# Where in a block of 512 bytes the high parts of one weight quarter begin: all four k-tiles at the stream's place, or the first two alone

## The chip, the core and the metric

The kernel runs on one core of one Trainium2 chip. The metric is the device time in microseconds of that core, from three executions: 716.06 us in the median, 715.36 to 717.12. A further execution was profiled and took 716.72 us; its span from the first to the last instruction is 714.9 us. All quoted times within the program are of that execution.

## The reference

The layer is one decoder block over 512 positions of width 1024, in float32. The half that the change touches is the feed-forward part:

```python
h = rmsnorm(x, norm2_g[l])
gu = h @ w_ffn_in[l]
g = causal_dwconv(gu[..., :D_FF], ffn_conv_w[l]) + ffn_conv_b[l]
x = x + (jax.nn.silu(g) * gu[..., D_FF:]) @ w_ffn_out[l]
```

with `D_FF = 2816`, so `w_ffn_in` is 1024 by 5632. Ahead of it stand a norm, an input projection, a short gated convolution, a sparse attention and a gated merge; the change touches nothing of them.

## The kernel before

**High and low parts.** TensorE reads each float32 operand as a rounded one (float32r). To keep accuracy, every operand is kept as a high part (the rounded value) and a low part (what is left), and every product is made of three matmuls: high weight by high data, high weight by low data, low weight by high data. `dense` (L400) issues, for one product over some k-tiles, first all pairs with the high weight (L403 with the high data, L404 with the low data, the same weights loaded for each) and then all with the low weight (L406). Each matmul has its own load of the stationary weights, a 128x128 block; the data stream through as the moving operand.

**The feed-forward part.** The 22 channel tiles of the gate and the 22 of the up projection are worked on in twos (`ff_strassen`). For two channel tiles and one of the two projections, `ff_forms` (L895) loads the two weight blocks and `ff_pair` (L939) makes the 2 by 2 block product in Strassen's form (Winograd's variant): seven products instead of eight, each of four k-tiles with half of the positions (256 columns). So one call of `ff_pair`, called a pair here, has 7 x 12 = 84 matmuls of 128x256, and there are 22 pairs. The data side, in seven combinations, lies ready in `xf_h` and `xf_l`. Of the weights, the lower right quarter (a22) is used as it is and has tiles of its own, `th` (high) and `tl` (low); a11 and a12 use a ring tile (`wh_s`, `wl_s`), and the four sums of quarters use `sh` and `sl`.

**The order in a pair.** The product with a22 comes first (called in L974): eight matmuls with `th`, two for each k-tile, and then four with `tl`. Then come a11, a12 and the sums. From the third pair on, two parts of the down projection (`pdn`, 24 matmuls of 128x512 each time) stand between one pair and the next, so that a pair is entered from the last matmuls of `pdn`.

**Where tiles lie.** The program sets every tile at a fixed byte in each partition. Written as the remainder by 512: the moving data `xf_h` and `xf_l` begin at 288, and since all their pieces are multiples of 512 bytes long, each stream of 256 columns begins at 288. The weights `tl`, `wh_s`, `wl_s`, `sh`, `sl` begin at 480, and each k-tile (128 columns, 512 bytes) likewise: 192 bytes further than the stream. The two buffers of `th` begin at 288, so that all four k-tiles of a22's high parts lie at the stream's place; a filler tile of 48 columns, `gap_w`, behind them takes the rest to 480. In `pdn` both sides lie at 480.

**Who makes the weights.** ScalarE writes `th` as a rounded copy of a22 and `tl` as its negative; a DMA of GpSimd's queue then adds the weights from memory onto `tl`, which leaves the rest (`dma_split`, L156). `p1` (L957, 256 columns) holds the product with a11: ScalarE copies it out of its bank (L976), and VectorE's first sum of the pair reads it (L954). It has two buffers. The order of instructions on every engine is set when the program is built, from the dependencies and a model of durations.

Of the kernel before, what the change touches and what calls it, by code (L numbers as in the profile page):

```python
# [11 lines left out]
F32 = mybir.dt.float32  # L12
F32R = mybir.dt.float32r
I32 = mybir.dt.int32
AF = mybir.ActivationFunctionType
ALU = mybir.AluOpType
AX = mybir.AxisListType

P = 128
D = 1024  # L20
# [62 lines left out]
def tile_block(ctx: ExitStack, tc: tile.TileContext, xT, pos, par, par2, w_tok, w_a3, w_gate, w_ao, w_bo, w_o,  # L83
               w_ff, w_dn, c_w1, out):
    nc = tc.nc
# [9 lines left out]
    def const(shape, name, dt=F32, pool=sb):  # L95
        return pool.tile(shape, dt, name=name, tag=name)
# [17 lines left out]
    def s_bank(name):  # L114
        return bank("s", name, 3)

    def t_bank(name):
        return bank("t", name, 2)

    def o_bank(name):  # L120
        return bank("o", name, 1)
# [29 lines left out]
    def split(h, l, v):  # L151
        hi = nc.scalar.activation(h, v, AF.Copy)  # L152
        nc.vector.tensor_sub(l, v, h.bitcast(F32))  # L153
        return hi

    def dma_split(h, l, raw, src, dst=None):  # L156

        nc.scalar.activation(h, raw, AF.Copy)  # L158
        nc.scalar.activation(l, raw, AF.Copy, scale=-1.0)  # L159
        nc.gpsimd.dma_start(l if dst is None else dst, src, accum_op=ALU.add)  # L160

    def ring(name):
        return (wf.tile([P, D], F32R, name=f"wh_{name}", tag="wh", bufs=NWF),
                wf.tile([P, D], F32R, name=f"wl_{name}", tag="wl", bufs=NWF))

    def raw_tile(name):
        return wf.tile([P, D], F32, name=f"wr_{name}", tag="wr", bufs=NRAW)
# [232 lines left out]
    def dense(acc, units, first=True, last=True):  # L400

        for i, (wh, wl, xh, xl) in enumerate(units):
            nc.tensor.matmul(acc, wh, xh, start=first and i == 0, stop=False)  # L403
            nc.tensor.matmul(acc, wh, xl, start=False, stop=False)  # L404
        for i, (wh, wl, xh, xl) in enumerate(units):
            nc.tensor.matmul(acc, wl, xh, start=False, stop=last and i == len(units) - 1)  # L406
# [412 lines left out]
    TH = S // 2  # L819
# [6 lines left out]
    xf_h = const([P, 4, 7, TH], "xf_h", F32R, px)  # L826
    xf_l = const([P, 4, 7, TH], "xf_l", F32R, px)
    pw = ctx.enter_context(tc.tile_pool(name="pw", bufs=1, side="left"))
    pw.tile([P, D // 2], F32R, name="th_", tag="th", bufs=2)
    const([P, 48], "gap_w", F32, pw)  # L830

    def x_forms(k, v):
# [6 lines left out]
    for n, j in enumerate(O_ORDER):  # L839
# [10 lines left out]
        k, half = j % 4, j // 4  # L850
        if half == 0:
            v = pc.tile([P, 7, TH], F32, name=f"xv{k}", tag="xv", bufs=2)
        nc.scalar.activation(v[:, 2 * half:2 * half + 2].rearrange("p a t -> p (a t)"), xj, AF.Copy,
                             scale=par_sb[:, G2 + j:G2 + j + 1])
# [38 lines left out]
    HALF_D = D // 2  # L893

    def ff_forms(f, n):  # L895

        nm = f"{n}_{f}"
        raws = []
        for m in range(2):
            raw = raw_tile(f"s{nm}{m}")  # L900
            nc.sync.dma_start(raw, w_ff[f + m, n])
            raws.append(raw)
        a11, a12 = raws[0][:, 0:HALF_D], raws[0][:, HALF_D:]
        a21, a22 = raws[1][:, 0:HALF_D], raws[1][:, HALF_D:]
        form = {}
        h = pw.tile([P, HALF_D], F32R, name=f"th{nm}", tag="th", bufs=2)
        l = pw.tile([P, HALF_D], F32R, name=f"tl{nm}", tag="tl", bufs=2)
        dma_split(h, l, a22, w_ff[f + 1, n][:, HALF_D:])
        form["a22"] = (h, l)
        h, l = ring(f"s{nm}")  # L910
        dma_split(h, l, raws[0], w_ff[f, n])
        form["a11"] = (h[:, 0:HALF_D], l[:, 0:HALF_D])
        form["a12"] = (h[:, HALF_D:], l[:, HALF_D:])

        def put(i, j, v):
            h = pw.tile([P, D], F32R, name=f"sh{i}{j}{nm}", tag="sh", bufs=NSQ)
            l = pw.tile([P, D], F32R, name=f"sl{i}{j}{nm}", tag="sl", bufs=NSQ)
            split(h, l, v)
            form[i] = (h[:, 0:HALF_D], l[:, 0:HALF_D])
            form[j] = (h[:, HALF_D:], l[:, HALF_D:])  # L920

        s = {}

        def pair(i, j):
            v = pw.tile([P, D], F32, name=f"s{i}{j}{nm}", tag="sf", bufs=NSF)
            s[i], s[j] = v[:, 0:HALF_D], v[:, HALF_D:]
            return v

        v = pair(2, 3)
        nc.vector.tensor_sub(s[3], a11, a21)  # L930
        nc.vector.tensor_sub(s[2], a22, s[3])
        put(2, 3, v)
        v = pair(4, 1)
        nc.vector.tensor_sub(s[4], a12, s[2])
        nc.vector.tensor_add(s[1], a21, a22)
        put(4, 1, v)
        return form

    def ff_pair(f, n, c, form, late=None):  # L939
        nm = f"{n}_{f}"  # L940
        b1, b26 = o_bank(f"p1{nm}"), t_bank(f"p26{nm}")
        b45, b37 = s_bank(f"p45{nm}"), s_bank(f"p37{nm}")
        lo, hi = slice(0, TH), slice(TH, S)

        def units(wf_, x, ks):
            wh, wl = form[wf_]
            return [(wh[:, k * P:(k + 1) * P], wl[:, k * P:(k + 1) * P], xf_h[:, k, x], xf_l[:, k, x]) for k in ks]

        def product(acc, wf_, x):
            dense(acc, units(wf_, x, range(4)))  # L950

        def sums(dst, bank, v):

            nc.vector.tensor_tensor(dst, bank.rearrange("p (a t) -> p a t", a=2), v[:, None, :].to_broadcast([P, 2, TH]),  # L954
                                    op=ALU.add)

        p1 = pw.tile([P, TH], F32, name=f"p1{nm}", tag="p1", bufs=2)  # L957
        c1, c2 = c[:, :, 0:TH], c[:, :, TH:]
        plan = [(b26, hi, 2, T2, True), (b37, hi, 3, T3, True), (b37, lo, 4, B22, False), (b45, hi, 1, T1, True),
                (b1, lo, "a11", B11, True), (b26, lo, "a12", B21, False), (b45, lo, "a22", T4, False)]  # L960
        if late is not None:

            for b, cols, wf_, x, opens in plan:
                for i, (wh, wl, xh, xl) in enumerate(units(wf_, x, range(3))):
                    for lhs, rhs, st in ((wh, xh, True), (wh, xl, False), (wl, xh, False)):
                        nc.tensor.matmul(b[:, cols], lhs, rhs, start=opens and st and i == 0, stop=False,
                                         skip_group_check=True)

            def product(acc, wf_, x):
                (wh, wl, xh, xl), = units(wf_, x, (3,))  # L970
                for lhs, rhs, last in ((wh, xh, False), (wh, xl, False), (wl, xh, True)):
                    nc.tensor.matmul(acc, lhs, rhs, start=False, stop=last, skip_group_check=True)

        product(b45[:, lo], "a22", T4)  # L974
        product(b1[:, lo], "a11", B11)
        nc.scalar.activation(p1, b1[:, lo], AF.Copy)  # L976
        product(b26[:, lo], "a12", B21)
        product(b26[:, hi], 2, T2)
        sums(c1, b26, p1)
        product(b37[:, hi], 3, T3)  # L980
        product(b37[:, lo], 4, B22)
        sums(c2, b37, c1[:, 1])
        product(b45[:, hi], 1, T1)
        sums(c[:, 1].rearrange("p (a t) -> p a t", a=2), b45, c2[:, 1])
        nc.vector.tensor_add(c2[:, 0], c2[:, 0], b45[:, hi])
# [3 lines left out]
    def ff_strassen(f, between):  # L989
        u = u_bufs[f // 2 % NU]  # L990

        with tc.high_priority(offset=AHEAD if f == 0 else 0):
            form = ff_forms(f, 0)
        ff_pair(f, 0, u[:, :, 2:], form, late=f == 0 or None)
        between()
        nc.vector.tensor_tensor(u[:, :, 2:], u[:, :, 2:], r2two, op=ALU.mult)
        cv = pair_tile(f"cv{f}", "cv")
        for m in range(2):
            conv_silu(f + m, cv[:, m], u[:, m])
        nc.vector.tensor_tensor(cv, cv, r2two, op=ALU.mult)  # L1000
        up = pair_tile(f"up{f}", "up")
        ff_pair(f, 1, up, ff_forms(f, 1))

        between()
        nc.vector.tensor_tensor(up, up, cv, op=ALU.mult)
        for m in range(2):
            h, l = a_tiles(f + m)
            split(h, l, up[:, m])
# [98 lines left out]
```

## Time and profile before

| What | Value |
|---|---|
| Time, median of three executions | 716.06 us (715.36 to 717.12) |
| Profiled execution: its own time, its span | 716.72 us, 714.9 us |
| TensorE busy | 708.9 us, 99% of the span, 4285 matmuls |
| ScalarE, VectorE, GpSimd busy | 432.6, 534.7, 181.9 us |
| Matmuls of 128x256 of the pairs | 84 x 22 = 1848, from 365 to 684 us |
| Granted TensorE clock, mean over the span | 0.999 |

Busy time of TensorE says little here: matmuls overlap in the records (a 128x256 one lasts 0.28 us, but the next starts 0.12 us later), so what a matmul costs is the distance from its start to the start of the next, called its step below. Steps can be read off the timeline, whose starts are given to 0.01 us, best over many matmuls at once. The duration of one matmul is a second reading: a matmul that was held up lasts some nanoseconds longer.

### The profile page before, as it was taken

The page shows a single profiled execution, that of the slowest core. Times are in us where ns is not written, and L with a number is a line of the kernel's source. Part 1 is how long each engine was busy: PE and PEld are TensorE (multiplying, and loading weights), DVE is VectorE, ACT ScalarE, POOL GpSimd, SP SyncE. Part 2 cuts the span into 40 slices and gives each one's busy share as a digit, 9 for nine tenths or more (in the row PEclk, how much of TensorE's full clock was granted, in tenths as well). Part 3 has the DMA queues.
Part 4 walks back from the last instruction along what each step waited for, and adds up shares of the span by engine and source line. Part 5 has one row for each costly group of instructions (what it writes and reads, how often), then busy time and mean ns, then how long its engine had stood idle before and what let it go on. Part 6 is the DMA issues. An engine that isn't in the chain of part 4 may idle for free.

```text
span 714.9 us, 11371 instructions
## 1 busy us (share of the span) xinstructions
PE 708.9 (99%) x4285; PEld 633.4 (89%) x4285; DVE 534.7 (75%) x957; ACT 432.6 (61%) x722; POOL 181.9 (25%) x179
## 2 busy tenths in 40 slices
PE   9999999999999999999999999999999999999997
PEld 9999777888888888888789999899999999999986
DVE  6887876687566878365795899988787877878643
ACT  7535655967667676522676776676565766646440
POOL 3151332133433334433012221221211222111110
PEclk9999999999999999999999999999999999999999
DMA  7333677611111122332676798987878778785665
GB/s 273 97 95 118 173 179 154 143 60 60 60 64 55 60 69 80 118 125 82 206 201 136 172 234 202 220 203 187 206 188 216 170 185 198 188 206 105 122 142 150
DMA packets 41142, 105.47 MB, mean 148 GB/s; under 512 B 3968, under 2 KB 9216, under 8 KB 41088
## 3 DMA queue, kind: packets, MB, share of 16 engines
q1 hardware_dynamic: 26528, 70.41, 29.9%
q0 software_dynamic: 14272, 34.08, 27.7%
q8 instruction: 33, 0.54, 0.3%
q10 hardware_dynamic: 288, 0.26, 0.1%
q14 instruction: 21, 0.17, 0.1%
HBM read 102.64 MB, written 2.10 MB: 147 GB/s over the span
## 4 chain that ended last, share of the span: by engine, by line
PE 95%; DMA 2%; ACT 1%; DVE 1%; issue 1%; POOL 1%; ACTq 0%; DVEq 0%; POOLq 0%; SPq 0%
PE p L404 9%; PE p L403 9%; PE p L406 9%; PE pdn L404 6%; PE pdn L403 6%; PE pdn L406 6%; PE pg L404 4%; PE pg L403 4%; PE pg L406 4%; PE pa L403 2%; PE pt L679 2%; PE pa L404 2%; PE pa L406 2%; PE po L403 2%; PE po L404 2%; PE pj_s L253 2%
## 5 line engine op out<-in xcount | busy, mean ns | idle before, releaser
L404 PE MATMUL p<-xf_l,sh 128*128 128x256 f32 x336 | 80.6, 277 | 0.0
L403 PE MATMUL p<-xf_h,sh 128*128 128x256 f32 x336 | 80.5, 277 | 0.0
L152 ACT ACTIVATE sh<-s 128x1024 fp32r<-128x1024 f32 x44 | 46.2, 1057 | 38.0 <-PE p L404 24.5
L404 PE MATMUL pdn<-al,wh_d 128*128 128x512 f32 x176 | 68.7, 391 | 0.0
L403 PE MATMUL pdn<-ah,wh_d 128*128 128x512 f32 x176 | 68.5, 390 | 0.0
L404 PEld LDWEIGHTS p<-xf_l,sh 128*128 128x128 f32 x336 | 63.0, 188 | 0.1
L403 PEld LDWEIGHTS p<-xf_h,sh 128*128 128x128 f32 x336 | 63.0, 188 | 0.1
L160 POOL DMA_DIRECT2D wl_s<-in_w_ff_dram x22 | 19.5, 885 | 166.8 <-ACT wl_s L159 155.6
L153 DVE TENSOR_TENSOR sl<-s,sh 128x1024 fp32r<-128x1024 f32 x44 | 53.6, 1221 | 8.7 <-ACT sh L152 8.7
L158 ACT ACTIVATE wh_s<-wr_s 128x1024 fp32r<-128x1024 f32 x22 | 23.3, 1059 | 53.1 <-PE pdn L404 50.3
L406 PE MATMUL p<-xf_h,sl 128*128 128x256 f32 x336 | 51.5, 277 | 0.0
L135 POOL TENSOR_TENSOR wl_g<-wr_g,wh_g 128x1024 fp32r<-128x1024 f32 x16 | 38.4, 2402 | 50.8 <-ACT wh_g L133 25.4
L403 PE MATMUL pg<-xg_h,wh_g 128*128 128x512 f32 x128 | 50.7, 396 | 0.0
L404 PE MATMUL pg<-xg_l,wh_g 128*128 128x512 f32 x128 | 50.6, 395 | 0.0
L406 PE MATMUL pdn<-ah,wl_d 128*128 128x512 f32 x176 | 47.7, 389 | 0.0
L160 POOL DMA_DIRECT2D wl_d<-in_w_dn_dram x22 | 26.5, 1203 | 77.9 <-ACT wl_d L159 69.8
L1026 DVE TENSOR_TENSOR x<-x,pdn 128x512 f32<-128x512 f32 x48 | 32.9, 685 | 16.2 <-PE pdn L406 15.5
L406 PEld LDWEIGHTS p<-xf_h,sl 128*128 128x128 f32 x336 | 44.5, 188 | 0.2
L403 PE MATMUL p<-xf_h,wh_s 128*128 128x256 f32 x168 | 40.5, 276 | 0.0
L404 PE MATMUL p<-xf_l,wh_s 128*128 128x256 f32 x168 | 40.4, 276 | 0.0
L406 PEld LDWEIGHTS pdn<-ah,wl_d 128*128 128x128 f32 x176 | 33.0, 188 | 6.9
L404 PEld LDWEIGHTS pdn<-al,wh_d 128*128 128x128 f32 x176 | 33.0, 188 | 6.2
(359 smaller groups left out, 2121.8 us busy)
## 6 DMA issues: line engine op xcount, KB each, us to landing
wr_s<-in_w_ff_dram SPq DMA_DIRECT2D x44, 512.0 KB, 5.0
wl_s<-in_w_ff_dram POOLq DMA_DIRECT2D x22, 512.0 KB, 7.8
wr_d<-in_w_dn_dram SPq DMA_DIRECT2D x22, 512.0 KB, 7.3
wl_d<-in_w_dn_dram POOLq DMA_DIRECT2D x22, 512.0 KB, 8.6
wr_g<-in_w_gate_dram SPq DMA_DIRECT2D x16, 512.0 KB, 3.4
wr_a<-in_w_a_dram SPq DMA_DIRECT2D x12, 512.0 KB, 4.3
tl<-in_w_ff_dram POOLq DMA_DIRECT2D x22, 256.0 KB, 7.6
wl_a<-in_w_a_dram POOLq DMA_DIRECT2D x10, 512.0 KB, 7.6
```

Source lines behind the costliest of these rows:

```text
L135: e.tensor_sub(lo[:, 0:n], raw[:, 0:n], hi[:, 0:n].bitcast(F32))
L152: hi = nc.scalar.activation(h, v, AF.Copy)
L153: nc.vector.tensor_sub(l, v, h.bitcast(F32))
L158: nc.scalar.activation(h, raw, AF.Copy)
L160: nc.gpsimd.dma_start(l if dst is None else dst, src, accum_op=ALU.add)
L253: nc.tensor.matmul(acc, xg_h[:, k, ts_], wh, start=k == 0, stop=False)
L403: nc.tensor.matmul(acc, wh, xh, start=first and i == 0, stop=False)
L404: nc.tensor.matmul(acc, wh, xl, start=False, stop=False)
L406: nc.tensor.matmul(acc, wl, xh, start=False, stop=last and i == len(units) - 1)
L679: nc.tensor.transpose(pt[:, i * P:(i + 1) * P], e[:, i, (kt + k0) * P:(kt + k0 + 1) * P], ident)
L1026: nc.vector.tensor_add(xj, xj, acc)
```

## The change

The buffers of `th` grow from 512 to 640 columns, and the high parts are written into them in two pieces: k-tiles 0 and 1 in the first 256 columns, then a hole of 48 columns (192 bytes), then k-tiles 2 and 3. With the buffers still beginning at 288, k-tiles 0 and 1 stay at the stream's place, and k-tiles 2 and 3 begin at 480, where all other weights of the pairs begin. The 1024 bytes that two larger buffers take are given back by `p1`, which has one buffer instead of two; everything between `th` and `p1` moves up by 1024 bytes, a multiple of 512. The call of `dma_split` is written out, since the high part's access now has two pieces and the low part's has one.

```diff
-    pw.tile([P, D // 2], F32R, name="th_", tag="th", bufs=2)
+    pw.tile([P, 5 * P], F32R, name="th_", tag="th", bufs=2)
     const([P, 48], "gap_w", F32, pw)
...
-        h = pw.tile([P, HALF_D], F32R, name=f"th{nm}", tag="th", bufs=2)
+        h = pw.tile([P, 5 * P], F32R, name=f"th{nm}", tag="th", bufs=2)
         l = pw.tile([P, HALF_D], F32R, name=f"tl{nm}", tag="tl", bufs=2)
-        dma_split(h, l, a22, w_ff[f + 1, n][:, HALF_D:])
+        step = 2 * P + 48
+        h = h[:, 0:2 * step].rearrange("p (a c) -> p a c", c=step)[:, :, 0:2 * P]
+        nc.scalar.activation(h, a22.rearrange("p (a c) -> p a c", a=2), AF.Copy)
+        nc.scalar.activation(l, a22, AF.Copy, scale=-1.0)
+        nc.gpsimd.dma_start(l, w_ff[f + 1, n][:, HALF_D:], accum_op=ALU.add)
         form["a22"] = (h, l)
...
-            return [(wh[:, k * P:(k + 1) * P], wl[:, k * P:(k + 1) * P], xf_h[:, k, x], xf_l[:, k, x]) for k in ks]
+            high = lambda k: wh[:, k // 2, k % 2 * P:(k % 2 + 1) * P] if wf_ == "a22" else wh[:, k * P:(k + 1) * P]
+            return [(high(k), wl[:, k * P:(k + 1) * P], xf_h[:, k, x], xf_l[:, k, x]) for k in ks]
...
-        p1 = pw.tile([P, TH], F32, name=f"p1{nm}", tag="p1", bufs=2)
+        p1 = pw.tile([P, TH], F32, name=f"p1{nm}", tag="p1", bufs=1)
```

The order of instructions is the same on all engines; only the access of one instruction differs, and, with the single buffer of `p1`, some of the waits. On ScalarE, around the a22 copy for the gate projection of channel tiles 8 and 9, it stands before (`p10_6` in the output is `p1` of an earlier pair, `th0_8` and `tl0_8` are a22's tiles, `wr_s0_81` the raw weights):

```order
L976 ACTIVATE p10_6_4709<-p10_6_4705 128x256
L891 ACTIVATE cv4_4500<-cv4_4500 128x512
L158 ACTIVATE th0_8_5016<-wr_s0_81_5014 128x512
L159 ACTIVATE tl0_8_5017<-wr_s0_81_5014 128x512
L158 ACTIVATE wh_s1_6_4855<-wr_s1_60_4846 128x1024
L159 ACTIVATE wl_s1_6_4856<-wr_s1_60_4846 128x1024
```

and with the change:

```order
L982 ACTIVATE p10_6_4709<-p10_6_4705 128x256
L892 ACTIVATE cv4_4500<-cv4_4500 128x512
L911 ACTIVATE th0_8_5016<-wr_s0_81_5014 128x2x256
L912 ACTIVATE tl0_8_5017<-wr_s0_81_5014 128x512
L158 ACTIVATE wh_s1_6_4855<-wr_s1_60_4846 128x1024
L159 ACTIVATE wl_s1_6_4856<-wr_s1_60_4846 128x1024
```

The copy to `th` stands in the same place and writes the same 512 columns, now as two runs of 256; nothing ahead of it or behind it has moved.

## The prediction

> **What bounds the kernel now.** I read first the page's busy times and its chain of waits:
>
> ```profile
> PE 708.9 (99%) x4285; PEld 633.4 (89%) x4285; DVE 534.7 (75%) x957; ACT 432.6 (61%) x722; POOL 181.9 (25%) x179
> PE 95%; DMA 2%; ACT 1%; DVE 1%; issue 1%; POOL 1%; ACTq 0%; DVEq 0%; POOLq 0%; SPq 0%
> ```
>
> TensorE is never short of work, and 95% of the chain that ends last is its own. So the steps of the matmuls, start to start, make the time. Next I read the groups of TensorE by shape, for the 205 us in which pairs and down projection alternate, and the sums of that window:
>
> ```profile
> L403 PE MATMUL p<-xf_h,sh 128*128 128x256 f32 x224 | 53.5, 276 | 0.0
> L404 PE MATMUL p<-xf_l,th 128*128 128x256 f32 x56 | 13.9, 282 | 0.0
> L403 PE MATMUL p<-xf_h,th 128*128 128x256 f32 x56 | 13.9, 281 | 0.0
> 478.90:683.90 205.00, 205.00 (x1490) 192.51 (x1489) 157.39 (x218) 121.87 (x161) 39.83 (x40) 1.00 0.77 179
> ```
>
> Here 224 matmuls, 16 of each pair, are 14 pairs. TensorE is busy for all 205 us at a granted clock of 1.00. With equal shapes, matmuls whose weights are `th`, at the stream's place, last 281 or 282 ns; those with weights 192 bytes further last 276. Taken alone, that says: move `th` away and gain. The timeline says more. One of the 14 pairs, from its first `th` to the first `pdn` behind it (columns: start, duration):
>
> ```profile
> 554.06 0.28 PE L403 MATMUL p<-xf_h,th 128*128 128x256 f32 x1
> 554.18 0.28 PE L404 MATMUL p<-xf_l,th 128*128 128x256 f32 x1
> 554.30 0.28 PE L403 MATMUL p<-xf_h,th 128*128 128x256 f32 x1
> 554.41 0.28 PE L404 MATMUL p<-xf_l,th 128*128 128x256 f32 x1
> 554.54 0.28 PE L403 MATMUL p<-xf_h,th 128*128 128x256 f32 x1
> 554.65 0.28 PE L404 MATMUL p<-xf_l,th 128*128 128x256 f32 x1
> 554.77 0.28 PE L403 MATMUL p<-xf_h,th 128*128 128x256 f32 x1
> 554.89 0.28 PE L404 MATMUL p<-xf_l,th 128*128 128x256 f32 x1
> 555.01 0.62 PE L406 MATMUL p<-xf_h,tl 128*128 128x256 f32 x4
> ...
> 563.62 0.39 PE L403 MATMUL pdn<-ah,wh_d 128*128 128x512 f32 x1
> ```
>
> And one earlier pair, in which seven of the eight `th` matmuls had run before some `pdn`, and one alone led into the rest:
>
> ```profile
> 464.39 0.28 PE L404 MATMUL p<-xf_l,th 128*128 128x256 f32 x1
> 464.51 0.63 PE L406 MATMUL p<-xf_h,tl 128*128 128x256 f32 x4
> ...
> 473.46 0.39 PE L403 MATMUL pdn<-ah,wh_d 128*128 128x512 f32 x1
> ```
>
> From the first `tl` to `pdn` both hold the same 76 matmuls, whose weights all lie at 192 bytes behind the stream. They take 563.62 - 555.01 = 8.61 us behind eight `th`, and 473.46 - 464.51 = 8.95 us behind one: steps of 113.3 and 117.8 ns. So the same instructions, at the same addresses, have two paces, and each keeps to the end of the pair. Traffic does not part them: the windows (columns: length, TensorE busy and count, clock, DMA share, GB/s)
>
> ```profile
> 409.20:417.70 8.50, 8.50 (x78) 1.00 1.02 264
> 464.51:473.46 8.95, 8.95 (x78) 1.00 0.98 223
> 555.01:563.62 8.61, 8.61 (x78) 1.00 0.69 137
> ```
>
> show 113 ns with the DMA engines at 1.02 as with 0.69, and 118 at 0.98. What parts them is how the stretch was entered:
>
> ```profile
> 397.71 0.28 PE L403 MATMUL p<-xf_h,th 128*128 128x256 f32 x1
> 397.83 0.28 PE L404 MATMUL p<-xf_l,th 128*128 128x256 f32 x1
> 397.95 1.10 PE L406 MATMUL p<-xf_h,sl 128*128 128x256 f32 x8
> 398.89 0.28 PE L403 MATMUL p<-xf_h,th 128*128 128x256 f32 x1
> ...
> 399.48 0.28 PE L404 MATMUL p<-xf_l,th 128*128 128x256 f32 x1
> 399.61 0.62 PE L406 MATMUL p<-xf_h,tl 128*128 128x256 f32 x4
> 438.05 0.63 PE L403 MATMUL pdn<-ah,wh_d 128*128 128x512 f32 x2
> 438.51 1.10 PE L406 MATMUL p<-xf_h,sl 128*128 128x256 f32 x8
> ```
>
> Eight `sl` that last 1.10 us have steps of (1.10 - 0.28) / 7 = 0.117 us: two `th` ahead did not help, nor did two `pdn`. Six `th` (398.89 to 399.48) did: the four `tl` last 0.62 us, steps of (0.62 - 0.28) / 3 = 0.113. So `th` at the stream's place costs a little itself, and it is also what brings TensorE into the close pace, for the 76 matmuls behind it.
>
> **The change part by part.**
>
> *k-tiles 2 and 3 moved.* The direct effect is on the fifth to eighth `th`: 555.01 - 554.54 = 0.47 us now. At 113.3 ns they would take 0.45, at 117.8 again 0.47. A gain of 0.02 us in each pair, or none: at most 0.4 us in 22 pairs.
>
> *Whether four still do it.* One and two fail, six and eight succeed; the trace has no clean entry with four. The steps within the eight decide for me. From the starts they are 0.12, 0.12, 0.11, 0.13, 0.11, 0.12, 0.12, 0.12: not settled after four, where the widest step is directly followed by the narrowest, and level only at the end. Six behind 398.89 end in a wide step as well, 0.13 (399.61 - 399.48), so a wide step alone proves neither. But the fourth's is followed by a `th` that is itself held up, whereas the close pace begins behind a run that had levelled. I take it that four are too few. Where a stretch is not brought into the close pace it was never seen to come in by itself: the 464.51 stretch kept 117.8 ns for 76 matmuls. What leads into the first `th` is always the settled end of `pdn`, so the 14 pairs should all go one way.
>
> The price then: 8.95 - 8.61 = 0.34 us for a pair, 14 x 0.34 = 4.8 us. Before these pairs the close pace also held in
>
> ```profile
> 399.60:408.10 8.50, 8.50 (x77) 1.00 0.55 147
> 430.30:438.00 7.70, 7.70 (x70) 1.00 0.85 203
> ```
>
> and in the window at 409.20 above: 24.7 us, at 113.3 ns 218 matmuls, by 4.5 ns each 1.0 us. These entries are less clean, so between 0 and 1.0; I take 1.0, since they too rest on six or eight `th`. The sum is 4.8 + 1.0 = 5.8 us, less the 0.0 of the four moved ones. It lies wholly on the path, since TensorE has no idle time to give. The bounds are -0.4 us (close pace kept) and +5.8 us. A slower TensorE makes the other engines' deadlines later, so nothing new comes due.
>
> *The copy in two runs, and `p1` in one buffer.*
>
> ```profile
> L158 ACT ACTIVATE th<-wr_s x22: 613/617/637, 354.5 to 646.8; 128x512 fp32r<-128x512 f32 x22
> L976 ACT ACTIVATE p<-p x22: 357/361/385, 389.8 to 677.2; 128x256 f32<-128x256 f32 x22
> 419.86 0.68 DVE L954 TENSOR_TENSOR up<-p,p 128x512 f32<-128x512 f32 x1
> 422.79 0.36 ACT L976 ACTIVATE p<-p 128x256 f32<-128x256 f32 x1
> ```
>
> The copy writes the same 512 columns; it costs nothing more if the hole is free, and at most as much as two copies of 256, 2 x 361 - 617 = 105 ns, 2.3 us in all on an engine that is idle for 39% of the span. The last copy runs at 646.8, and the last `th` matmuls start at 675, 28 us later; even without that cover, 105 ns in 22 pairs would be 2.3 us. With one buffer, the write of `p1` waits for VectorE's read of the pair before; queued behind it on ScalarE are the copies that make weights. The closest case is the one above: the read ends at 420.54 and the write starts at 422.79, 2.25 us of room. Both edits cost nothing; no DMA is added, moved or resized, and no other remainder by 512 changes.
>
> **The rivals.**
>
> *Four are enough.* For it: the fourth `th` ends in a wide step, as the eighth does, and the shift comes in a rhythm that could have the same place after four as after eight. Against it: the fifth step is narrow although its weights still lie at the stream's place, and is followed by more wide ones, so the walk goes on. It would give 14 to 22 pairs x 0.02 us = 0.3 to 0.4 us less, 715.7 us. This is the one that ends on the other side. It decides by the step behind the fifth `th`: 113 ns there and in the 76 behind.
>
> *Only the clean pairs go wide, or the pace comes in late.* If a pair found the close pace halfway, it would lose 0.17 us, 14 x 0.17 = 2.4, and up to 0.5 us before: 718.5 to 719. Against it: no stretch at 117.8 ns was seen to come in without `th` or `pdn` ahead.
>
> *The addresses do nothing.* If the two paces came from something else, moving half of `th` would leave 716.1 us. Against it: 281 and 282 against 276 ns in the same 14 pairs. The Trainium skill, "TensorE: Matmul & The Clock Gate", section "Step-by-step: what each phase is for", states this rule: TensorE has two independent read ports, and loading the next weights takes no read bandwidth from the running matmul. By that rule no byte offset of a weight could matter, and the time would stay at 716.1 us. The trace speaks against it here, with 5 to 6 ns by offset alone.
>
> **How the numbers follow.** The profiled execution's 716.72 us would become 722.5; it stands 0.66 us above the median, so against the median of 716.06 the forecast is 716.06 + 5.8 = 721.9 us (own range 720.5 to 723.2: the 1.0 us of the early stretches may stay, and the runs shown spread by 1.8 us). Chances: four are too few 0.72; four are enough 0.20, at 715.7; the middle case 0.05, at 718.5 to 719; no effect 0.03. The range over these, so that no more than two in ten are left out, is 715.3 to 723.2 us. About 0.3%, 2.1 us, is what a measurement of this kernel can tell from no change. Slower by more: 0.72 and most of the middle case, 0.76. Faster by more would need the stretches that are wide now to come in as well. The longest are the 8.95 us above and
>
> ```profile
> 390.50:397.70 7.20, 7.20 (x63) 1.00 0.84 157
> 423.10:428.00 4.90, 4.90 (x42) 1.00 0.95 295
> ```
>
> 21 us in all; 4.5 ns of each 117.8 would be 0.8 us, with the 0.4 of `th` 1.2 us, under the bound: 0.02. The same: 0.22.
>
> **What would show it.** In the window of the 14 pairs, the groups with `sh`, `sl`, `wh_s`, `wl_s` and `tl` lasting 279 to 280 ns instead of 276, and 76 matmuls from the first `tl` to `pdn` in 8.95 us instead of 8.61, show the main step right; 276 and 8.61 show it wrong, and the rival right. The `th` groups of the second half at 279 or 280 go with it, at 276 with the rival. `pdn` should keep 388 to 391 ns. New idle time of ScalarE behind `p1`, or of TensorE at all, would show that the two small edits were mispriced. The forecast falls if the fifth `th` of a pair already steps by 113 ns.

## The result and the profile after

The changed kernel takes 722.33 us in the median of five executions (721.55 to 724.71); the kernel before took 716.33 us beside it (715.36 to 717.12). The ratio is 1.0085, with an interval of 1.0070 to 1.0099: slower by 6.0 us, 0.8%. The forecast was 721.9 us, with an own range of 720.5 to 723.2.

The profiled execution took 722.33 us, its span 720.6 us, 5.7 more than before. The page's busy times and its chain:

```profile
PE 714.1 (99%) x4285; PEld 638.2 (89%) x4285; DVE 535.3 (74%) x957; ACT 432.9 (60%) x722; POOL 182.4 (25%) x179
PE 95%; DMA 2%; DVE 1%; POOL 0%; ACT 0%; issue 0%; ACTq 0%; DVEq 0%; SPq 0%
```

TensorE is busy for 5.2 us more, with the same 4285 matmuls; VectorE, ScalarE and GpSimd stand within 0.6 us of before. The groups of TensorE from 480 to 690 us, which hold the 14 clean pairs (84 matmuls in one piece, each behind a whole `pdn`), and the sums of these pairs' window (length, TensorE busy and count, and at the end clock, DMA share, GB/s):

```profile
L403 PE MATMUL p<-xf_h,sh 128*128 128x256 f32 x224 | 55.3, 280 | 0.0
L404 PE MATMUL p<-xf_l,th 128*128 128x256 f32 x56 | 13.8, 280 | 0.0
L403 PE MATMUL pdn<-ah,wh_d 128*128 128x512 f32 x105 | 41.1, 392 | 0.0
479.89:689.64 209.75, 209.75 (x1490) 197.09 (x1489) 157.66 (x218) 122.12 (x161) 39.84 (x40) 1.00 0.76 175
```

`sh` lasted 276 ns before and lasts 280 now, although neither its place by 512 nor its order has changed. The window is 209.75 us long instead of 205.00, still without a gap in TensorE and at a clock of 1.00. One pair in the timeline (start, duration), its first `th`, the fifth to the eighth, `tl` and the first `pdn` behind it:

```profile
556.75 0.28 PE L403 MATMUL p<-xf_h,th 128*128 128x256 f32 x1
...
557.23 0.28 PE L403 MATMUL p<-xf_h,th 128*128 128x256 f32 x1
557.34 0.28 PE L404 MATMUL p<-xf_l,th 128*128 128x256 f32 x1
557.46 0.28 PE L403 MATMUL p<-xf_h,th 128*128 128x256 f32 x1
557.57 0.28 PE L404 MATMUL p<-xf_l,th 128*128 128x256 f32 x1
557.69 0.63 PE L406 MATMUL p<-xf_h,tl 128*128 128x256 f32 x4
...
566.64 0.40 PE L403 MATMUL pdn<-ah,wh_d 128*128 128x512 f32 x1
```

From the first `tl` to `pdn` the 76 matmuls take 566.64 - 557.69 = 8.95 us: the wide pace, 117.8 ns. The fifth `th`, the first one 192 bytes behind the stream, steps by 557.34 - 557.23 = 0.11 us. That is one close step; the three behind it, up to the first `tl`, take 557.69 - 557.34 = 0.35 us, 0.117 each, the wide pace.

Where the 5.7 us lie can be read off the first `th` of the first and of the last clean pair, in the timelines of before and of after:

```profile
478.93 0.28 PE L403 MATMUL p<-xf_h,th 128*128 128x256 f32 x1
674.27 0.28 PE L403 MATMUL p<-xf_h,th 128*128 128x256 f32 x1
```

```profile
479.92 0.28 PE L403 MATMUL p<-xf_h,th 128*128 128x256 f32 x1
679.68 0.28 PE L403 MATMUL p<-xf_h,th 128*128 128x256 f32 x1
```

The 14 pairs begin 0.99 us later than before. From the first to the last, 13 periods of a pair and its `pdn`, there are 195.34 us before and 199.76 after, 15.03 and 15.37 for each: 4.42 us more. The fourteenth pair adds 0.34. The sum is 0.99 + 4.42 + 0.34 = 5.75 us.

Of the 0.99 us ahead of them, 0.90 arise behind the first matmul of the pairs, which starts at 365.29 us before and at 365.38 now: they belong to the early stretches. All three that the prediction counted now begin with four `tl` at the wide pace, (0.63 - 0.28) / 3 = 0.117:

```profile
399.56 0.63 PE L406 MATMUL p<-xf_h,tl 128*128 128x256 f32 x4
409.44 0.63 PE L406 MATMUL p<-xf_h,tl 128*128 128x256 f32 x4
431.09 0.63 PE L406 MATMUL p<-xf_h,tl 128*128 128x256 f32 x4
```

### The profile page after: what moved, and what is told of

Read it like the earlier page. It is cut to its first block, busy times and chain, and to the rows that moved or that the text cites. A ratio compares the mean times of both kernels' runs of the same rounds, so it can differ in the third digit from the quotient of the medians.

```text
span 720.6 us, 11387 instructions
## 1 busy us (share of the span) xinstructions
PE 714.1 (99%) x4285; PEld 638.2 (89%) x4285; DVE 535.3 (74%) x957; ACT 432.9 (60%) x722; POOL 182.4 (25%) x179
## 4 chain that ended last, share of the span: by engine, by line
PE 95%; DMA 2%; DVE 1%; POOL 0%; ACT 0%; issue 0%; ACTq 0%; DVEq 0%; SPq 0%
PE p L403 10%; PE p L406 10%; PE p L404 10%; PE pdn L403 6%; PE pdn L404 6%; PE pdn L406 6%; PE pg L404 4%; PE pg L403 4%; PE pg L406 4%; PE pa L406 3%; PE pa L403 3%; PE pa L404 3%; PE pt L679 2%; PE po L403 2%; PE po L404 2%; PE pj_s L253 2%
## 5 line engine op out<-in xcount | busy, mean ns | idle before, releaser
L403 PE MATMUL p<-xf_h,sh 128*128 128x256 f32 x336 | 82.6, 280 | 0.0
L404 PE MATMUL p<-xf_l,sh 128*128 128x256 f32 x336 | 82.6, 279 | 0.0
L403 PEld LDWEIGHTS pdn<-ah,wh_d 128*128 128x128 f32 x176 | 33.0, 188 | 6.3
```

## The experiments

The theory of the prediction: out of the settled `pdn` (its 24 matmuls in one piece, with weights at the stream's place, as in the kernel before), a pair reaches the close pace only through a long run of matmuls whose weights lie at the stream's place, and four are too few. Its rivals: each matmul has its own price by its own offset (then moving `th` away gains); the loss comes from a side effect of the edit (the copy in two runs, the single `p1`, moved tiles). All times are medians of several executions, each beside executions of the kernel before on the same chip. "At the stream" counts the a22 matmuls of a pair whose weights lie at the stream's place.

| Kernel | At the stream, of 12 | Weights of `pdn` | Time, us | Ratio to before (interval) | Clean pairs at the wide pace |
|---|---|---|---|---|---|
| before | 8 | at the stream | 716.0 to 716.7 | 1 | 0 of 14 |
| the change | first 4 | at the stream | 722.33 | 1.0085 (1.0070 to 1.0099) | 14 |
| 1 no hole | 8 | at the stream | 716.33 | 1.0001 (0.9991 to 1.0011) | 0 |
| 2 all away | 0 | at the stream | 721.53 | 1.0076 (1.0061 to 1.0091) | 14 |
| 3 three k-tiles | first 6 | at the stream | 722.30 | 1.0090 (1.0070 to 1.0110) | 14 |
| 4 the two last | 4, later | at the stream | 721.63 | 1.0073 (1.0056 to 1.0090) | 14 |
| 7 eight, mixed | first 4 `th`, 4 `tl` | at the stream | 716.79 | 1.0008 (0.9996 to 1.0019) | 0 |
| 5 `pdn` away | 8 | 192 behind | 720.31 | 1.0055 (1.0040 to 1.0070) | 10 |
| 6 nothing at the stream | 0 | 192 behind | 716.84 | 1.0006 (0.9997 to 1.0016) | 0 |
| 8 four, `pdn` away | first 4 | 192 behind | 719.77 | 1.0043 (1.0025 to 1.0061) | 7 |
| 9 low data at the stream | 0 | 192 behind; with `al` at the stream | 723.73 | 1.0108 (1.0089 to 1.0126) | 14 |

The last column is counted from the mean step of the 72 matmuls behind the product with a22, pair by pair in the traces: it is 113.3 or 117.8 ns in every one of the 14 pairs of each kernel, never between. In kernels 3, 4 and 7 the order of some matmuls ahead of the 14 pairs differs from before too, so there the pace of the pairs says more than the total.

**1. The edit without the hole.** Everything of the change stays, the larger buffers, the copy with an access in two pieces, the single `p1`; the second piece follows the first directly.

```diff
-        step = 2 * P + 48
+        step = 2 * P
```

> The changed kernel with its larger tile, its copy written out as two runs and its single buffer of p1, but without the hole of 48 columns: all four k-tiles of th are at the stream's place again. Lead-in theory (eight th at the stream's place bring TensorE into the close pace, four do not): as before, 716 us, tl and sums lasting 276 ns. Side-effect theory (the single buffer of p1 or the written-out copy made the time): as the changed kernel, 722 us.

Measured: 716.33 us, the time before. Its groups from 480 to 690 us:

```profile
L403 PE MATMUL p<-xf_h,sh 128*128 128x256 f32 x224 | 53.6, 277 | 0.0
L404 PE MATMUL p<-xf_l,th 128*128 128x256 f32 x52 | 12.9, 282 | 0.0
```

`sh` is back at 277 ns, `th` at 282. So the loss is the hole, that is the place of k-tiles 2 and 3, and nothing beside it.

**2. All of `th` away.** From the kernel before; the filler lies ahead of `th` instead of behind it, so that all eight matmuls have weights 192 bytes behind the stream.

```diff
-    pw.tile([P, D // 2], F32R, name="th_", tag="th", bufs=2)
     const([P, 48], "gap_w", F32, pw)
+    pw.tile([P, D // 2], F32R, name="th_", tag="th", bufs=2)
```

> The kernel before with the filler ahead of th instead of behind it: all four k-tiles of th lie 192 bytes behind the stream, nothing else is touched. Lead-in theory: no pair is brought into the close pace, so all 76 matmuls of the 14 pairs step by 117.8 ns: 716.3 + 4.8 + 1.0 - 0.0 = 722 us, like the changed kernel. Direct-cost theory (a matmul at the stream's place costs some 6 ns and nothing else): 176 x 6 ns less, 715.3 us.

Measured: 721.53 us. A pair of it, from the first `tl` to `pdn`:

```profile
556.92 0.63 PE L406 MATMUL p<-xf_h,tl 128*128 128x256 f32 x4
565.87 0.40 PE L403 MATMUL pdn<-ah,wh_d 128*128 128x512 f32 x1
```

565.87 - 556.92 = 8.95 us, the wide pace. That each matmul has its own price by its own offset falls: with the dearer offset gone, the time goes up by 5.5 us. Half a run at the stream's place is no better than none.

**3 and 4. Six, and four elsewhere.** Kernel 3 puts the hole behind the third k-tile, with the copy written as two instructions; kernel 4 is the change with a22's k-tiles taken in the order 2, 3, 0, 1, so that the four at the stream's place stand directly ahead of `tl`.

```diff
-        step = 2 * P + 48
-        h = h[:, 0:2 * step].rearrange("p (a c) -> p a c", c=step)[:, :, 0:2 * P]
-        nc.scalar.activation(h, a22.rearrange("p (a c) -> p a c", a=2), AF.Copy)
+        h0, h1 = h[:, 0:3 * P], h[:, 3 * P + 48:4 * P + 48]
+        nc.scalar.activation(h0, a22[:, 0:3 * P], AF.Copy)
+        nc.scalar.activation(h1, a22[:, 3 * P:], AF.Copy)
...
+            high = lambda k: wh[:, k * P + 48 * (k > 2):(k + 1) * P + 48 * (k > 2)] if wf_ == "a22" else wh[:, k * P:(k + 1) * P]
```

> The changed kernel with the hole behind the third k-tile: six th matmuls at the stream's place, two away. Lead-in theory: the steps of the eight level only at the seventh, so six from the settled end of pdn are too few: 722 us. If the number needed is between four and six: 716 us. Side-effect theory: 722 us too, so this run places the threshold only if it comes out at 716.

```diff
-            dense(acc, units(wf_, x, range(4)))
+            dense(acc, units(wf_, x, (2, 3, 0, 1) if wf_ == "a22" else range(4)))
```

> The changed kernel with the k-tiles of a22 taken in the order 2, 3, 0, 1, so that the four matmuls at the stream's place come last, next to the tl that follow. Lead-in theory: a run of four is too short wherever it stands: 722 us, tl and sums lasting 279 to 280 ns. Rival that only the last matmuls ahead of the rest count: 716 us and 276 ns.

Measured: 722.30 and 721.63 us. A pair of kernel 3 and one of kernel 4:

```profile
556.68 0.64 PE L406 MATMUL p<-xf_h,tl 128*128 128x256 f32 x4
565.64 0.40 PE L403 MATMUL pdn<-ah,wh_d 128*128 128x512 f32 x1
```

```profile
557.34 0.64 PE L406 MATMUL p<-xf_h,tl 128*128 128x256 f32 x4
566.29 0.39 PE L403 MATMUL pdn<-ah,wh_d 128*128 128x512 f32 x1
```

Both wide: 8.96 and 8.95 us. Six in a run are too few out of the settled `pdn`, and four are too few behind four others as well as ahead of them. Seven, and more than eight, were not tried.

**7. Eight, made of others.** The change, but `tl` lies at the stream's place too, and its four matmuls are issued between the `th` of k-tiles 1 and 2: eight in a run, of which four are low weights.

```diff
     pw.tile([P, 5 * P], F32R, name="th_", tag="th", bufs=2)
+    pw.tile([P, D // 2], F32R, name="tl_", tag="tl", bufs=2)
     const([P, 48], "gap_w", F32, pw)
...
+            u = units(wf_, x, range(4))
+            ops = [(wh, xx) for wh, _, xh, xl in u[:2] for xx in (xh, xl)] + [(wl, xh) for _, wl, xh, _ in u]
+            ops += [(wh, xx) for wh, _, xh, xl in u[2:] for xx in (xh, xl)]
+            for i, (lhs, rhs) in enumerate(ops):
+                nc.tensor.matmul(acc, lhs, rhs, start=i == 0, stop=i == 11)
```

`tl` stands ahead of the filler now and so begins at the same remainder as `th`.

> The changed kernel (th of k-tiles 2 and 3 away, one buffer of p1), but with tl at the stream's place, and the four tl matmuls directly behind the four th of k-tiles 0 and 1: again a run of eight at the stream's place, made of other weights. The four th of k-tiles 2 and 3 follow. Lead-in theory (length of the run decides, not whose weights): close pace, 716.3 us, sums lasting 276 ns. If it were a matter of the k-tiles 2 and 3 of th themselves, or of the side effects: 722 us, 279 to 280 ns.

Measured: 716.79 us. Its groups from 480 to 690 us, and a pair behind its eight:

```profile
L403 PE MATMUL p<-xf_h,sh 128*128 128x256 f32 x224 | 53.5, 276 | 0.0
L964 PE MATMUL p<-xf_h,tl 128*128 128x256 f32 x52 | 8.3, 282 | 0.0
```

```profile
555.12 0.28 PE L403 MATMUL p<-xf_h,wh_s 128*128 128x256 f32 x1
563.27 0.39 PE L403 MATMUL pdn<-ah,wh_d 128*128 128x512 f32 x1
```

Now `tl` lasts 282 ns and `sh` 276. The 72 matmuls from the first `wh_s` on take 8.15 us, 113.2 ns each. The hole is still there, and the loss is gone: it is the eight at the stream's place out of the settled `pdn` that count, not whose weights make them. Eight that are not in a row were not tried.

**5. `pdn` away too.** From the kernel before; a filler of 192 bytes moves `ah` and `al`, so that the weights of `pdn` lie 192 bytes behind its stream as well. The eight `th` stay at the stream's place.

```diff
+    const([P, 48], "gap_a", F32, pf)
     u_bufs = []
```

> The kernel before with ah and al, the moving side of the down projection, 192 bytes lower, so that its weights lie 192 bytes behind the stream as in the pairs; th stays at the stream's place. pdn steps by 227 ns now, 13.6 over 512 columns at 2.4 a ns; the pairs step by 6.6 over in the close pace and 11.1 in the wide one. If pdn keeps the close pace of the pair ahead of it, 528 x 6.9 ns = 3.6 us less, 712.5 us; if it goes wide, 528 x 2.4 = 1.3 us less, 714.8 us, and the next pair's eight th start from the wide pace; if these do not bring it in then, 5.8 us more, 720.6 us.

Measured: 720.31 us. That lies beside the third case of the expectation, 720.6, but by luck: `pdn` did not get faster, and ten of the 14 pairs went wide, not all. Three neighbouring pairs, first `tl` and first `pdn` of each, and a group of `pdn` from 480 to 690 us:

```profile
525.63 0.63 PE L406 MATMUL p<-xf_h,tl 128*128 128x256 f32 x4
534.58 0.40 PE L403 MATMUL pdn<-ah,wh_d 128*128 128x512 f32 x1
541.03 0.64 PE L406 MATMUL p<-xf_h,tl 128*128 128x256 f32 x4
549.99 0.39 PE L403 MATMUL pdn<-ah,wh_d 128*128 128x512 f32 x1
556.43 0.62 PE L406 MATMUL p<-xf_h,tl 128*128 128x256 f32 x4
565.05 0.39 PE L403 MATMUL pdn<-ah,wh_d 128*128 128x512 f32 x1
```

```profile
L403 PE MATMUL pdn<-ah,wh_d 128*128 128x512 f32 x108 | 42.3, 392 | 0.0
```

8.95, 8.96, 8.62 us: two wide pairs and a close one, and so on in threes through all 14. So eight in a run bring TensorE into the close pace every time when it comes out of the settled `pdn`, and one time in three here. The instructions of the three have the same form and the same remainders by 512. The pair before may leave a state that passes through the 24 matmuls of `pdn`; that is argued, not shown (see kernel 8).

**6. Nothing at the stream's place.** Kernels 2 and 5 together: no weight of the feed-forward part lies at the stream's place.

> As the run with pdn away, and th away as well: in the whole feed-forward part no weight lies at the stream's place. Lead-in theory: nothing brings TensorE in, or it is in by the entry and stays: pairs wide, 279 to 280 ns, about 720 us. Direct-cost theory: 3.6 and 1.1 us less than before, 711.6 us.

Measured: 716.84 us, not told from before. A pair of it with the end of the `pdn` ahead (its last four matmuls), and two groups:

```profile
552.73 1.08 PE L406 MATMUL pdn<-ah,wl_d 128*128 128x512 f32 x4
553.64 0.28 PE L403 MATMUL p<-xf_h,th 128*128 128x256 f32 x1
554.55 0.62 PE L406 MATMUL p<-xf_h,tl 128*128 128x256 f32 x4
563.16 0.39 PE L403 MATMUL pdn<-ah,wh_d 128*128 128x512 f32 x1
568.66 0.28 PE L403 MATMUL p<-xf_h,th 128*128 128x256 f32 x1
```

```profile
L403 PE MATMUL p<-xf_h,sh 128*128 128x256 f32 x224 | 53.5, 276 | 0.0
L404 PE MATMUL p<-xf_l,th 128*128 128x256 f32 x52 | 12.4, 277 | 0.0
```

The pair is close from its first step: eight `th` in 554.55 - 553.64 = 0.91 us instead of 0.95, the 76 behind in 8.61. This refutes one half of the theory: a run at the stream's place is not the only way in. Out of a `pdn` that lies 192 bytes behind its stream itself, a pair is in the close pace without any. The gain is 0.04 us a pair, and `pdn` takes it back: its 24 matmuls last 568.66 - 563.16 = 5.50 us, against 5.47 before, where the next pair begins at

```profile
569.09 0.28 PE L403 MATMUL p<-xf_h,th 128*128 128x256 f32 x1
```

and `pdn` at the 563.62 shown in the prediction.

**8. The change behind such a `pdn`.** The filler of kernel 5 in the changed kernel.

> The change, and pdn's weights moved 192 bytes behind its stream too. Theory 'the entry alone decides': a pair that comes out of such a pdn is in the close pace already (as when no weight lay at the stream's place), four th do not take it out again: all 14 pairs at 113.3 ns, 716 to 717.5 us. Theory 'a run at the stream's place sets the phase anew, and only eight of them end in the close pace': four leave the 14 pairs wide, 14 x 0.34 = 4.8 us and about 1 us before them, 721 to 723.5 us. If the state is handed on from pair to pair, as with eight th behind this pdn (two wide pairs, then a close one), something between, 718.5 to 721.

Measured: 719.77 us. Two neighbouring pairs, first `th` and first `pdn` of each:

```profile
524.14 0.28 PE L403 MATMUL p<-xf_h,th 128*128 128x256 f32 x1
534.04 0.39 PE L403 MATMUL pdn<-ah,wh_d 128*128 128x512 f32 x1
539.54 0.28 PE L403 MATMUL p<-xf_h,th 128*128 128x256 f32 x1
549.08 0.39 PE L403 MATMUL pdn<-ah,wh_d 128*128 128x512 f32 x1
```

The 84 matmuls take 9.90 us in the one and 9.54 in the other, and so in turns through all 14. Seven wide pairs by 0.34 us are 2.4 us of the 3.1 measured. It is the third case of the expectation, with a period of two here and three in kernel 5. That a state is handed on from pair to pair would fit it, but a rival stands untested: gate and up projection alternate, with two buffers of `th`, and the weight ring of pairs and `pdn` has three buffers and serves both once for each pair, so that other things of the kernel return after two and after three pairs as well. Against this rival alone, the kernel before and kernel 6 rotate the same buffers, and all their 14 pairs go one way. In this surrounding four at the stream's place leave fewer pairs wide than eight do, 7 against 10.

**9. How much of `pdn` has to lie away.** Kernel 2, with a filler that moves `ah` alone: the matmuls with `ah` have weights 192 bytes behind, those with `al` keep them at the stream's place. Each bank still ends in four matmuls that lie 192 behind.

```diff
+    pf.tile([P, S], F32R, name="ah_", tag="ah", bufs=NA)
+    const([P, 48], "gap_a", F32, pf)
     a_tiles(0)
```

> All th 192 bytes behind the stream; in pdn the stream of ah moved so that its matmuls have weights 192 bytes behind, while those with al keep them at the stream's place. Each bank of pdn ends in four matmuls 192 behind (low weights), and the two banks' high parts alternate 192 and 0. Theory 'the last few pdn matmuls decide': the pairs are entered close, sh and tl last 276 to 277 ns, and with 8 of 24 pdn matmuls back at the stream's place pdn's mean step is at most that of all away (229 ns): 715.5 to 717 us. Theory 'the whole of pdn has to run 192 behind': the pairs are entered as from the settled pdn, 117.8 ns, sh and tl 279 to 280 ns: 721 to 723 us.

Measured: 723.73 us, the slowest of all, and 0.7 above the second theory's 721 to 723. A pair and the `pdn` behind it, and the group of `pdn`'s low weights:

```profile
556.67 0.28 PE L403 MATMUL p<-xf_h,th 128*128 128x256 f32 x1
566.56 0.40 PE L403 MATMUL pdn<-ah,wh_d 128*128 128x512 f32 x1
572.14 0.28 PE L403 MATMUL p<-xf_h,th 128*128 128x256 f32 x1
```

```profile
L406 PE MATMUL pdn<-ah,wl_d 128*128 128x512 f32 x104 | 28.5, 397 | 0.0
```

The pairs are wide (9.89 us), and `pdn` takes 5.58 us instead of 5.47, which the theory did not have. The last four matmuls of each bank, at the same offset as in kernel 6, last 397 ns here. So four at that offset, behind this `pdn`, are not enough to enter the pair in the close pace. That `pdn` has two paces of its own, and that the pair takes over which of them it meets, would fit kernels 6 and 9; it was not tested further.

No kernel beats the one before. Close pairs throughout and a `pdn` at 5.47 us would be worth some 22 x 0.04 = 0.9 us; low weights of `pdn` alone 192 behind might give it; it was not tried.

## Why the prediction was right, step by step

**The main term, 14 x 0.34 = 4.8 us,** came out as forecast: all 14 pairs went wide, 8.95 us for the 76 matmuls against 8.61, 4.42 + 0.34 = 4.76 us by the starts. `pdn`, expected at 388 to 391 ns, has a group at 392. That the price lies in matmuls which the edit doesn't touch is what the trace of before already showed, in its one pair with a single `th` ahead.

**The early stretches, 1.0 us of a bound from 0 to 1.0:** measured 0.90 us from the first matmul of the pairs to the first clean pair. The beginnings of the three stretches are shown wide above.

**The four moved `th`, 0.0 us:** the fifth to the eighth take 557.69 - 557.23 = 0.46 us, before 0.47.

**The small edits at nothing:** shown by kernel 1, 1.0001 with an interval of 0.9991 to 1.0011, and by ScalarE's groups in the changed kernel, 620 ns for the copy in two runs and 2.4 us of idle time ahead of `p1` in all, against 1.9 before:

```profile
L911 ACT ACTIVATE th<-wr_s 128x512 fp32r<-128x512 f32 x22 | 13.6, 620 | 5.9 <-DMA wr_s<-in_w_ff_dram 5.7
L982 ACT ACTIVATE p<-p 128x256 f32<-128x256 f32 x22 | 8.1, 366 | 2.4 <-PE p L406 2.4
```

That idle time ended with TensorE's product, not with VectorE's read of the single buffer.

**"Four are enough"** came true for one step. The prediction said that the forecast falls if the fifth `th` already steps by 113 ns. It does, and the forecast did not fall: the next steps are wide again. The sign was wrongly drawn; a pace shows only over several steps, and the 76 behind were the right measure. Kernels 3 and 4 bear out that four, and even six, are too few. But the reason by which the prediction chose against this rival does not hold, and that its choice came true is luck. It read the steps off starts rounded to 0.01 us, as not settled after four and level after eight. Taken to the nanosecond from the same trace, as means over the 14 pairs, the eight steps are 116, 118, 119, 121 and again 117, 118, 120, 121 ns, and only the ninth is 113. The second four repeat the first to within 1 ns, as the rival had said of its rhythm: the steps hold no sign that anything levels between the fourth and the eighth. Why eight lead in and four do not stays open.

**"Six did",** which the prediction read from the early stretch behind 398.89, doesn't hold in general: out of the settled `pdn` six fail (kernel 3). That stretch was entered another way, out of eight `sl` at the wide pace. The forecast needed only that four fail.

**"What brings TensorE into the close pace"** was too wide as a cause. It holds out of a `pdn` at its stream's place, where eight bring it in, and zero, four and six don't. Behind another `pdn` eight bring it in only every third time, and none at all does so every time (kernels 5 and 6). Neither of the two expectations built on the wider claim came true in its mechanism. The sum of the prediction was not touched, since the change leaves `pdn` where it is.

**The addresses do nothing** is refuted by the kernel before against kernel 2, which differ in the place of tiles alone: 5.5 us. The rule of the Trainium skill named in the prediction ("TensorE: Matmul & The Clock Gate", section "Step-by-step: what each phase is for"), that loading the next weights takes no read bandwidth from the running matmul, would have left 716.1 us; the kernels whose 14 pairs all go wide differ from it by 5.5 to 7 us, by offsets alone.

## What to carry to other kernels

A matmul's price can lie in the matmuls behind it: before moving an operand that looks dear in its own row, look in the timeline for the same instructions at two paces, and for what each was entered from. Price such a change by the whole stretch that follows, and count how often it is entered in the same way, since the gain or loss comes in whole stretches. An offset that helps in one surrounding can harm in another (eight at the stream's place are worth 5.5 us behind one `pdn` and cost 3.5 us behind the other), so try both neighbours together. And do not rank single steps by starts that are rounded to 0.01 us; take the mean over many like stretches.

## What was not expected of the hardware

- Matmuls of 128x256 whose weights lie 192 bytes behind the stream have two paces, 113.3 and 117.8 ns, at a clock of 1.00 and with the same instructions; a pair keeps one of them for 72 matmuls or more, and none of the 14 pairs of any run lay between.
- Behind a `pdn` whose weights lie 192 bytes behind its stream, close and wide pairs come in turns, with a period of three in kernel 5 and of two in kernel 8. Whether a state outlives the 24 matmuls of `pdn`, or the rotation of buffers does it, is not shown.
- For 128x512, weights 192 behind the stream are a little dearer than at its place (5.50 against 5.47 us for 24), and both offsets mixed are dearer than either (5.58).
- What makes the two paces is open: the runs show which entries lead to which, not what in TensorE or its memory keeps them.
